# Gate products in seven-product form from output block 2 on, with the scaled sums of x made during attention in a buffer of their own

## The chip, the cores and the metric

The kernel runs on one core of one Trainium2 chip. The metric is the time of one execution on the device in microseconds (us). The five engines of a core (PE for matrix products, DVE and ACT for elementwise work, POOL for elementwise work and for issuing DMAs, SP for issuing DMAs) each work through a queue of their own in order and wait for each other by semaphores. Sixteen DMA engines move data between the core's memory and the device memory.

## The reference

One residual block of a streaming encoder, on x of 512 positions by 1024 channels, in float32:

```python
h = rms_norm(x, norm_mix_g[l])
proj = h @ w_in[l]
cb, cc, cin, q, k, v, f_logit, g_logit = jnp.split(proj, split_idx, axis=-1)
u = causal_dwconv(cc * cin, conv_mix_w[l])
y_conv = (cb * u) @ w_out_conv[l]
log_f = jax.nn.log_sigmoid((f_logit + b_f[l]).astype(jnp.float32))
o = forgetting_attention(q, k, v, log_f)
y_attn = o @ w_out_attn[l]
gates = jax.nn.sigmoid(g_logit + b_gate[l])
g_conv, g_attn = jnp.split(gates, 2, axis=-1)
x = x + (g_conv * y_conv + g_attn * y_attn) @ w_o[l]
h = rms_norm(x, norm_ffn_g[l])
up = causal_dwconv(h @ w_up[l], conv_ffn_w[l])
a, b = jnp.split(up, 2, axis=-1)
x = x + (jax.nn.silu(a) * b) @ w_down[l]
return rms_norm(x, norm_f_g)
```

The change touches `g_logit`, the last 2048 of the columns of `h @ w_in`: two gates for each of 1024 channels.

## The kernel before

Everything lies transposed: channels on the 128 partitions, the 512 positions along the free axis, so x is eight tiles of 128 by 512 (`KB` = 8). Each float32 operand is split into a high and a low part (`xgh` and `xgl` for x times the norm's gain, `wh` and `wl` for a weight block), and a product is three passes: high by high, low weight by high, high weight by low (`mm3`, L308). A pass over 128 by 512 outputs is two matmuls of 256 columns. The factor of the norm that depends on the position, `rb1`, is multiplied in when a result leaves PSUM.

The stages follow each other: the loads of x and of the v weights with the v product (a loop over the eight x tiles, `kb`), the q and k projections of two head pairs, attention (32 units of scores, softmax and transposes, with the remaining projections put between them as filler), the gate stage (a loop over eight output blocks `j`), the product with `w_o`, the channel mixer's up and down products and the last norm.

**The gate stage.** Output block `j` needs two gates of 128 channels each (`ga`, `gb`), the products `yc` and `ya` of the two branches (`chunk("mix…")`, 48 matmuls), and then gates times branches, which gives `mh` and `ml`. For `j` below `GJ` = 3 the two gates are two plain projections, 48 matmuls each (for `j` = 0 they were already made during attention). From `j` = 3 on the two gates of a block are one 2 by 2 block product with seven instead of eight block products (`seven`, L326): two steps of 42 matmuls. Such a step takes one load `P` of three weight blocks for each product pair, which come ready, and one load `F` of four sums of weight blocks. The sums are made in device memory by accumulating DMAs (`make_forms`): for each group of steps three copies issued on SP (L207) and three accumulations issued on POOL (L210), at counted slots during attention. `GATES` lists the steps, ten of them.

The seven products also need sums of x blocks. For these, x is loaded once more in float32 into `xt` (four DMAs of 512 KB on POOL's queue, L856). `x_scale` multiplies by the gain (ACT, L863), `x_sums` makes four sums and differences in place (DVE, L871 to L876), and `x_split` makes the high and low parts `xth` and `xtl` (ACT L882, DVE L883). These are entries of the list `later`: a piece with the index of a weight chunk from which it may run, an estimated DVE time and names by which a user can demand it. `split()` prepares the high and low parts of the next weight chunk (ACT L274, DVE L278), two chunks ahead of their use, and then runs pieces of `later` that fit a budget.

**Buffers.** The left side of the core's memory holds long-lived tiles, then `abp` (`xgh`, `xgl`, and the branch outputs). The right side holds `ap` during attention, and afterwards `xp`, `hp` and `mp` in the same place. The tag `x1` in `xp` is first `xt`; at `j` = 7 it becomes `x1`, x in float32 for the residual (four DMAs on POOL, L954), to which L1079 adds each block of the `w_o` product. The gates and their intermediate sums take turns in six buffers `mt`. PSUM has eight banks; `ring` hands out banks in turn, and `seven` takes four named ones.

**What sets the order.** Matmuls and instructions wrapped in `keep` stay in the order of the program. The rest is put in an order by the framework's scheduler, and each engine then runs its list strictly in that order, so a piece of work may stand at another place of an engine's list than the text suggests.

Of the kernel before, what the change touches and what calls it, by code (L numbers as in the profile page):

```python
# [8 lines left out]
F32 = mybir.dt.float32  # L9
F32R = mybir.dt.float32r  # L10
AF = mybir.ActivationFunctionType
ALU = mybir.AluOpType

P = 128
D = 1024
S = 512
KB = D // P
# [17 lines left out]
G1, G2, GF, BG, CM, CF, BF = 0, 8, 16, 24, 40, 52, 184  # L35
# [17 lines left out]
)  # L53
HELD = 2

GJ = 3
GATES = tuple(((j, q), (j, q + 1)) for j in range(GJ, KB) for q in (0, 2))

PLAIN = [(m, k) for m in (6, 7) for k in range(*PHASES[1])]
# [11 lines left out]
def block_kernel(ctx, tc, xT, vecs, wv, win, wmix, wo, wup, wst, wdp, outT):  # L71
# [3 lines left out]
    nc = tc.nc  # L75
# [25 lines left out]
    def col(i):  # L101
        return vec[:, i : i + 1]
# [22 lines left out]
    stream = [(f"v{kb}", wv[kb], S + H) for kb in range(KB)]  # L125
# [28 lines left out]
    raws, parts, order = [], [], {}  # L154
    pools = {"raw": wp}
    later = []
# [143 lines left out]
    def mm3(out, wh, wl, xh, xl, start, stop):  # L300


        n = out.shape[-1]
        cut = [slice(a, a + 2 * P) for a in range(0, n, 2 * P)] if n > 2 * P else [slice(0, n)]
        trio = ((wh, xh), (wl, xh), (wh, xl))
        for i, (w, x) in enumerate(trio):
            for c, cs in enumerate(cut):
                keep(nc.tensor.matmul(  # L308
                    out[:, cs], w, x[:, cs],
                    start=start and i == 0 and c == 0,  # L310
                    stop=stop and i == 2 and c == len(cut) - 1,
                ))
# [67 lines left out]
    otl = abp.tile([P, 4, S], F32R, tag="otl", name="otl")  # L380
    ych = abp.tile([P, 4, S], F32R, tag="ych", name="ych")
    ycl = abp.tile([P, 4, S], F32R, tag="ycl", name="ycl")

    at = ExitStack()
    ap = at.enter_context(tc.tile_pool(name="ap", bufs=1, side="right"))
# [61 lines left out]
    for kb in range(KB):  # L447
# [13 lines left out]
        for cs in cuts:  # L461
            keep(nc.vector.scalar_tensor_tensor(
                xgl[:, kb, cs], x[:, cs], col(G1 + kb), xgh.bitcast(F32)[:, kb, cs],
                op0=ALU.mult, op1=ALU.subtract,
# [33 lines left out]
    def proj(idx, name, evac, bank):  # L498
        st = {}

        def half(i):
            if i == 0:
                st["w"] = chunk(f"in{idx}")
                st["p"] = bank(f"p_{name}")
            wh, wl = st["w"]
            for kb in range(4 * i, 4 * i + 4):
                ks = slice(kb * P, (kb + 1) * P)
                mm3(st["p"], wh[:, ks], wl[:, ks], xgh[:, kb, :], xgl[:, kb, :], kb == 0, kb == KB - 1)
            if i == 1:

                while len(parts) < chunk.n + 2:
                    split()
                with after_split():
                    evac(st["p"])

        return [lambda: half(0), lambda: half(1)]
# [151 lines left out]
    def run_all(fs):  # L668
        for f in fs:
            f()  # L670
# [70 lines left out]
    run_all(proj(17, "k1", evac_qk(1, False), ring(1)))  # L741
    acc, bank_s, bank_t = ring(2, 0, 1), ring(3, 4), ring(5, 6)

    fill = []
    gp = []
    for idx in late:
        kind, i = divmod(idx, 4)
# [32 lines left out]
    def split_next():  # L780
        if len(parts) == chunk.n and stream[chunk.n][0] not in ("dp1", "dp2"):
            split()
# [38 lines left out]
            split_next()  # L821


    acc = ring(3, 4, 5, 6, 0, 1, 2, 7)
    xp = ctx.enter_context(tc.tile_pool(name="xp", bufs=1, side="right"))
    xt = xp.tile([P, KB, S], F32, tag="x1", name="xt")
    xth = xp.tile([P, KB, S], F32R, tag="x1h", name="xth")
    xtl = xp.tile([P, KB * S + PADR], F32R, tag="x1l", name="xtl")[:, : KB * S]
    xtl = xtl.rearrange("p (a b) -> p a b", b=S)

    hg = ExitStack()
    hp = hg.enter_context(tc.tile_pool(name="hp", bufs=1, side="right"))
# [5 lines left out]
    mp = mg.enter_context(tc.tile_pool(name="mp", bufs=1, side="right"))  # L838
    pools["rg"] = mp

    def mt(name):
        return mp.tile([P, S], F32, tag="mt", name=name, bufs=6)

    def evac_gate(idx, dst):
        def f(p):
            g = mt(f"g{idx}")
            nc.vector.tensor_mul(g, p, rb1)
            nc.scalar.activation(g, g, AF.Sigmoid, bias=col(BG + idx))
            dst.append(g)

        return f

    for q in range(4):
        nc.gpsimd.dma_start(xt[:, 2 * q : 2 * q + 2, :], xT[:, 2 * q : 2 * q + 2, :])  # L856
    xq = xt.rearrange("p (q b) (h c) -> p q (b h) c", b=2, h=2)
    xqh, xql = (t.rearrange("p (q b) (h c) -> p q (b h) c", b=2, h=2) for t in (xth, xtl))

    def x_scale(q):  # L860
        def f():
            for kb in (2 * q, 2 * q + 1):
                nc.scalar.activation(xt[:, kb, :], xt[:, kb, :], AF.Copy, scale=col(G1 + kb))  # L863

        return f

    def x_sums(qs):
        b11, b12, b21, b22 = (xq[:, qs, i, :] for i in range(4))

        def f():  # L870
            nc.vector.tensor_sub(b11, b11, b12)  # L871
            nc.vector.tensor_sub(b12, b22, b12)

        def g():
            nc.vector.scalar_tensor_tensor(b22, b11, -1.0, b22, op0=ALU.mult, op1=ALU.subtract)
            nc.vector.scalar_tensor_tensor(b21, b22, -1.0, b21, op0=ALU.mult, op1=ALU.subtract)  # L876

        return f, g

    def x_split(q):  # L880
        def f():
            nc.scalar.activation(xqh[:, q], xq[:, q], AF.Copy)  # L882
            nc.vector.tensor_sub(xql[:, q], xq[:, q], xqh.bitcast(F32)[:, q])  # L883

        return f

    k = [c[0] for c in stream].index("mix1")
    for q in (0, 2):
        f, g = x_sums(slice(q, q + 2))
        for i in (q, q + 1):  # L890
            later.append((k, 0, (("q", i),), x_scale(i)))
        later.append((k, 1.4, (("q", q),), f))
        later.append((k, 1.5, (("q", q),), g))
        for i in (q, q + 1):
            later.append((k + 1, 1.25, (("q", i),), x_split(i)))
        k += 2

    def gate_form(q, g):
        if g < 3:
# [47 lines left out]
    for j in range(KB):  # L947
        gs = []
        for _ in range(3):
            slot()  # L950
        if j == KB - 1:
            x1 = xp.tile([P, KB, S], F32, tag="x1", name="x1")
            for q in range(4):
                nc.gpsimd.dma_start(x1[:, 2 * q : 2 * q + 2, :], xT[:, 2 * q : 2 * q + 2, :])  # L954
        if j == 0:
            evac_gate(0, gs)(gp[0])
            evac_gate(8, gs)(gp[1])
        elif j < GJ:
            run_all(proj(20 + j, f"ga{j}", evac_gate(j, gs), acc))
            run_all(proj(28 + j, f"gb{j}", evac_gate(8 + j, gs), acc))  # L960
        else:
            if j == GJ:
                acc = ring(2, 7, 3, 4)
            seven(GATES[2 * (j - GJ) : 2 * (j - GJ) + 2], 2 * (j - GJ), {j: (0, 1, 5, 6)}, gate_form, done=gate_pair(j, gs))
        wh, wl = chunk(f"mix{j}")
        yc, ya = acc(f"yc{j}"), acc(f"ya{j}")
        for pp, hh, ll, o in ((yc, ych, ycl, 0), (ya, oth, otl, 4)):
            for k in range(4):
                ks = slice((o + k) * P, (o + k + 1) * P)
                mm3(pp, wh[:, ks], wl[:, ks], hh[:, k, :], ll[:, k, :], k == 0, k == 3)  # L970
        if j >= GJ:
            split_next()
            flush()
        a, b = gs
        nc.vector.tensor_mul(a, a, yc)
        nc.vector.tensor_mul(b, b, ya)
        nc.gpsimd.tensor_add(a, a, b)
        nc.scalar.activation(mh[:, j, :], a, AF.Copy)
        nc.vector.tensor_sub(ml[:, j, :], a, mh.bitcast(F32)[:, j, :])

    assert not todo_bg
    mg.close()
    ab.close()
    gx = ctx.enter_context(tc.tile_pool(name="gx", bufs=1))
    gx.tile([P, PADL], F32, tag="pad", name="pad_g")
    gh = gx.tile([P, NG, 2 * P], F32R, tag="gh", name="gh")
# [6 lines left out]
    acc = ring(0, 1, 5, 6, 3, 4, 2, 7)  # L993
# [80 lines left out]
    for j in range(KB):  # L1074
        slot()
        if j == 0:
            po = lead(["wo0", "wo1"], mh, ml)
        p = po[j] if j < 2 else block(f"wo{j}", mh, ml)
# [4 lines left out]
            op0=ALU.mult, op1=ALU.subtract,  # L1083
# [23 lines left out]
    acc = turns(0, 1, *(2, 3, 4, 5) * 2, 6, 7, 0, 1, 2, 3, 4, 5)  # L1107
# [185 lines left out]
    for ph, (j0, j1) in enumerate(PHASES):  # L1293
        if ph:
            flush()
            acc = turns(*X * 5)
# [211 lines left out]
```

## Time and profile before

| what | value |
|---|---|
| median of 3 runs | 696.33 us (696.13 to 696.6) |
| the profiled execution's own time | 695.75 us |
| its span, first to last instruction | 693.9 us |
| granted clock of PE in it | 0.998 |
| DVE, ACT, POOL busy | 531.4, 359.2, 178.3 us |

The span is 1.85 us shorter than the time of the same execution; what lies around it belongs to the launch. Sums below are made against the span and then carried to the median. In a profile, L with a number is a line of the kernel, `out<-in` names what is written and read, and the names of an engine with a small q (SPq, ACTq) are its queue of issues. A matmul row's duration is longer than the distance to the next matmul, because matmuls overlap; distances are read from starts or from counts in a window.

### The profile page before, as it was taken

The numbers are of one execution on the slowest core, as the hardware profiler recorded it, in microseconds if no ns is written. First come the engines' busy times: TensorE is split into PE (matmuls) and PEld (weight loads), VectorE is DVE, ScalarE is ACT, GpSimd is POOL, SyncE is SP. The second block draws the span as 40 slices with busy tenths as digits, with TensorE's granted clock in tenths as the row PEclk, the third lists the DMA queues.
The fourth block names the chain that finished last, engine by engine and source line by source line (L and its number), as shares of the span: only waits on it lengthen the run. The fifth ranks groups of instructions, "written<-read, shape, count | busy, mean of one in ns | idle before, by whom it ended". The sixth has DMA issues, their size and how long they took to land.

```text
span 693.9 us, 14635 instructions
## 1 busy us (share of the span) xinstructions
PE 686.2 (99%) x5972; PEld 684.6 (99%) x5972; DVE 531.4 (77%) x826; ACT 359.2 (52%) x565; POOL 178.3 (26%) x194
## 2 busy tenths in 40 slices
PE   9999999999999999999999999999999999999996
PEld 9999999999999999999999999999999999999996
DVE  6677877776577778768879799888774677777894
ACT  5665655644565444446554455545443344445572
POOL 4134846532221201113513134210000313222000
PEclk9999999999999999999999999999999999999999
DMA  7528988543698596766899776355646686776513
GB/s 256 158 70 272 197 200 193 129 91 92 223 263 244 166 269 193 207 217 141 114 316 294 201 178 135 116 177 176 201 128 232 141 195 157 188 169 172 164 31 122
DMA packets 58387, 124.68 MB, mean 180 GB/s; under 512 B 5280, under 2 KB 26800, under 8 KB 58320
## 3 DMA queue, kind: packets, MB, share of 16 engines
q1 hardware_dynamic: 40776, 99.68, 44.5%
q0 software_dynamic: 16304, 22.88, 20.9%
q10 hardware_dynamic: 1240, 1.19, 0.5%
q8 instruction: 47, 0.77, 0.4%
q14 instruction: 20, 0.16, 0.1%
HBM read 121.57 MB, written 39.32 MB: 232 GB/s over the span
## 4 chain that ended last, share of the span: by engine, by line
PE 96%; DVE 3%; issue 0%; ACT 0%; DVEq 0%
PE dn L326 24%; PE p_up L308 21%; PE p_in L308 14%; PE p_up L326 6%; PE p_wo L308 6%; PE yc L308 3%; PE ya L308 3%; PE pa L472 2%; PE pb L474 2%; PE p_q L308 2%; PE p_k L308 2%; PE p_gb L308 2%; PE p_ga L308 2%; PE o L653 2%; PE tp L636 1%; PE pdB L308 1%
## 5 line engine op out<-in xcount | busy, mean ns | idle before, releaser
L308 PE MATMUL p_up<-x1h,wh_up 128*128 128x256 f32 x464 | 90.5, 276 | 0.0
L308 PE MATMUL p_up<-x1h,wl_up 128*128 128x256 f32 x464 | 90.4, 276 | 0.0
L308 PE MATMUL p_up<-x1l,wh_up 128*128 128x256 f32 x464 | 90.3, 276 | 0.0
L308 PEld LDWEIGHTS p_up<-x1h,wh_up 128*128 128x128 f32 x464 | 69.9, 188 | 0.0
L308 PEld LDWEIGHTS p_up<-x1h,wl_up 128*128 128x128 f32 x464 | 69.9, 188 | 0.0
L308 PEld LDWEIGHTS p_up<-x1l,wh_up 128*128 128x128 f32 x464 | 69.8, 188 | 0.0
L274 ACT ACTIVATE wh_up<-raw_up 128x1024 fp32r<-128x1024 f32 x38 | 40.2, 1057 | 49.6 <-PE p_up L308 43.0
L210 POOL DMA_DIRECT2D f<-in_wst_dram x57 | 65.5, 1309 | 0.1
L278 DVE TENSOR_TENSOR wl_F<-raw_F,wh_F 128x1024 fp32r<-128x1024 f32 (+1 forms) x36 | 47.8, 1328 | 18.5 <-ACT wh_F L274 18.2
L308 PE MATMUL p_in<-xgh,wh_in 128*128 128x256 f32 x288 | 56.8, 279 | 0.0
L308 PE MATMUL p_in<-xgh,wl_in 128*128 128x256 f32 x288 | 56.6, 278 | 0.0
L308 PE MATMUL p_in<-xgl,wh_in 128*128 128x256 f32 x288 | 56.5, 278 | 0.0
L278 DVE TENSOR_TENSOR wl_up<-raw_up,wh_up 128x1024 fp32r<-128x1024 f32 x38 | 47.1, 1240 | 12.1 <-ACT wh_up L274 12.1
L274 ACT ACTIVATE wh_F<-raw_F 128x1024 fp32r<-128x1024 f32 (+1 forms) x36 | 37.9, 1053 | 35.4 <-PE dn L326 27.8
L1206 POOL TENSOR_TENSOR ge<-fu,fu 128x512 f32<-128x512 f32 x11 | 18.8, 1706 | 141.6 <-DVE fu L565 117.6
L274 ACT ACTIVATE wh_P<-raw_P 128x768 fp32r<-128x768 f32 (+1 forms) x36 | 30.0, 834 | 31.6 <-PE dn L326 22.3
L278 DVE TENSOR_TENSOR wl_P<-raw_P,wh_P 128x768 fp32r<-128x768 f32 (+1 forms) x36 | 35.0, 972 | 13.7 <-ACT wh_P L274 9.1
L308 PEld LDWEIGHTS p_in<-xgh,wh_in 128*128 128x128 f32 x288 | 44.7, 188 | 0.7
L326 PE MATMUL dn<-gl,wh_F 128*128 128x256 f32 x192 | 45.1, 276 | 0.0
L326 PE MATMUL dn<-gh,wh_F 128*128 128x256 f32 x192 | 45.1, 276 | 0.0
L308 PEld LDWEIGHTS p_in<-xgl,wh_in 128*128 128x128 f32 x288 | 43.7, 188 | 0.0
L308 PEld LDWEIGHTS p_in<-xgh,wl_in 128*128 128x128 f32 x288 | 43.6, 188 | 0.0
(349 smaller groups left out, 2148.5 us busy)
## 6 DMA issues: line engine op xcount, KB each, us to landing
raw_up<-in_wup_dram SPq DMA_DIRECT2D x38, 512.0 KB, 4.2
raw_F<-f SPq DMA_DIRECT2D x35, 512.0 KB, 4.5
raw_P<-in_wst_dram SPq DMA_DIRECT2D x35, 384.0 KB, 4.9
raw_in<-in_win_dram SPq DMA_DIRECT2D x26, 512.0 KB, 3.5
f<-in_wst_dram POOLq DMA_DIRECT2D x35, 256.0 KB, 6.4
f<-in_wst_dram SPq DMA_DIRECT2D x17, 512.0 KB, 5.7
f<-in_wst_dram POOLq DMA_DIRECT2D x17, 512.0 KB, 8.0
f<-f SPq DMA_DIRECT2D x34, 256.0 KB, 5.4
```

The source lines that it names most:

```text
L210: return lambda: keep(nc.gpsimd.dma_start(dst, src, accum_op=ALU.add))
L274: ins = nc.scalar.activation(hi, raw, AF.Copy)
L278: ins = nc.vector.tensor_sub(lo, raw, hi.bitcast(F32))
L308: keep(nc.tensor.matmul(out[:, cs], w, x[:, cs], start=start and i == 0 and c == 0, stop=stop and i == 2 and c == len(cut) - 1,))
L326: keep(nc.tensor.matmul(out, wl if x == 1 else wh, xl if x == 2 else xh, start=opens and bk not in seen, stop=closes and bk not in left,))
L472: keep(nc.tensor.matmul(pa[t][:, :VW], xt, w[:, VB:], start=start, stop=stop))
L474: keep(nc.tensor.matmul(pb[t], xt, w[:, :VB], start=start and t % 2 == 0, stop=stop and t % 2 == 1))
L636: keep(nc.tensor.transpose(tp[:, ks], pt[:, ks], ident))
L653: keep(nc.tensor.matmul(o[:, 2 * P * e + c0 : 2 * P * (e + 1)], w, x[:, kb, c0:], start=e == 0 and kb == 0 and i == 0, stop=e == 1 and kb ...
L1206: keep(nc.gpsimd.tensor_mul(ge, a.rearrange(halves_of, h=2), b.rearrange(halves_of, h=2)))
```

## The change

`GJ` goes from 3 to 2, so the two gates of output block 2 become two steps of seven products too (`GATES` now has twelve steps). `xt` gets a buffer of its own, 16 KB per partition in a new pool `yp` on the left side, open from before attention to the end of the gate stage. Its four loads and the pieces `x_scale` and `x_sums` are written ahead of attention, with chunk indices during attention; `x_split` stays behind attention and is set for the chunks of block 0. The place that was `xt` becomes `xm`, whose eight slices serve in turn as the gates' buffers instead of the six `mt`; since `x1` has the same tag, its loads now stand behind the gate loop. Two rings of PSUM banks are changed to go with it.

```diff
-GJ = 3
+GJ = 2
@@ -381,6 +381,10 @@
+    yg = ExitStack()
+    yp = yg.enter_context(tc.tile_pool(name="yp", bufs=1))
+    xt = yp.tile([P, KB, S], F32, tag="xt", name="xt")
@@ -740,6 +744,39 @@
+    for q in range(4):
+        nc.gpsimd.dma_start(xt[:, 2 * q : 2 * q + 2, :], xT[:, 2 * q : 2 * q + 2, :])
...
+    k = len(parts) + 2
+    for q in (0, 2):
+        f, g = x_sums(slice(q, q + 2))
+        for i in (q, q + 1):
+            later.append((k + i - q, 0, (("q", i),), x_scale(i)))
+        later.append((k + 2, 1.4, (("q", q),), f))
+        later.append((k + 3, 1.5, (("q", q),), g))
+        k += 4
@@ -821,12 +858,13 @@
-    acc = ring(3, 4, 5, 6, 0, 1, 2, 7)
+    acc = ring(3, 4, 5, 6, 2, 7)
-    xt = xp.tile([P, KB, S], F32, tag="x1", name="xt")
+    xm = xp.tile([P, KB, S], F32, tag="x1", name="xm")
@@ -839,7 +877,10 @@
-        return mp.tile([P, S], F32, tag="mt", name=name, bufs=6)
+        mt.n += 1
+        return xm[:, (mt.n - 1) % KB, :]
+
+    mt.n = 0
@@ -884,16 +900,9 @@
-    k = [c[0] for c in stream].index("mix1")
-    for q in (0, 2):
-        f, g = x_sums(slice(q, q + 2))
-        for i in (q, q + 1):
-            later.append((k, 0, (("q", i),), x_scale(i)))
-        later.append((k, 1.4, (("q", q),), f))
-        later.append((k, 1.5, (("q", q),), g))
-        for i in (q, q + 1):
-            later.append((k + 1, 1.25, (("q", i),), x_split(i)))
-        k += 2
+    k = [c[0] for c in stream].index("mix0")
+    for q in range(4):
+        later.append((k + q // 2, 1.25, (("q", q),), x_split(q)))
@@ -948,10 +957,6 @@
-        if j == KB - 1:
-            x1 = xp.tile([P, KB, S], F32, tag="x1", name="x1")
-            for q in range(4):
-                nc.gpsimd.dma_start(x1[:, 2 * q : 2 * q + 2, :], xT[:, 2 * q : 2 * q + 2, :])
...
-                acc = ring(2, 7, 3, 4)
+                acc = ring(3, 4, 2, 7)
@@ -980,7 +985,11 @@
+    yg.close()
     ab.close()
+    x1 = xp.tile([P, KB, S], F32, tag="x1", name="x1")
+    for q in range(4):
+        nc.gpsimd.dma_start(x1[:, 2 * q : 2 * q + 2, :], xT[:, 2 * q : 2 * q + 2, :])
```

The loads of `xt`, `x_scale` and `x_sums` stand in the second piece and leave their old place ahead of the fifth.

Where the scheduler puts the moved pieces is read from the order of each engine's list.

**POOL at the program's start**, where it clears the attention's operand tiles (`qb`, `kb`) and then waits to compute the norm's factor `rc_n`. Before:

```order
L527 MEMSET qb_110 4x512
L526 MEMSET kb_111 64x512
L525 MEMSET kb_112 4x512
L527 MEMSET kb_111 4x512
L526 MEMSET kb_112 64x512
L527 MEMSET kb_112 4x512
L355 TENSOR_TENSOR rc_n_415<-ms_n_413,ex 128x4
```

Now:

```order
L531 MEMSET qb_114 4x512
L530 MEMSET kb_115 64x512
L529 MEMSET kb_116 4x512
L531 MEMSET kb_115 4x512
L530 MEMSET kb_116 64x512
L749 DMA xt<-in_xT_dram 128x1024
L531 MEMSET kb_116 4x512
L749 DMA xt<-in_xT_dram 128x1024 x3
L355 TENSOR_TENSOR rc_n_419<-ms_n_417,ex 128x4
```

The four loads of `xt` stand among the clears, ahead of the norm's factor, in the stage that loads x and the v weights; no instruction in front of them waits for another engine there.

**POOL at the end of the gate stage**, where it adds the two gated branches of a block (`xm`, before `ga`), issues accumulations for the sums of the up weights (`f`) and then sums squares (`ssq`). Before, with the last rows of the stage:

```order
L210 DMA f_2593<-in_wst_dram 256x1x512
L954 DMA x_3803<-in_xT_dram 128x1024 x4
L977 TENSOR_TENSOR g_2928<-g_2928,g_2986 128x512
L977 TENSOR_TENSOR ga_3161<-ga_3161,gb_3166 128x512
L210 DMA f_2591<-in_wst_dram 256x1x256
L210 DMA f_2592<-in_wst_dram 256x1x256
L210 DMA f_2593<-in_wst_dram 256x1x256
L977 TENSOR_TENSOR ga_3351<-ga_3351,gb_3356 128x512
L977 TENSOR_TENSOR ga_3540<-ga_3540,gb_3545 128x512
```

Now:

```order
L210 DMA f_2618<-in_wst_dram 256x1x256
L982 TENSOR_TENSOR xm<-xm 128x512
L210 DMA f_2619<-in_wst_dram 256x1x256
L210 DMA f_2620<-in_wst_dram 256x1x256
L982 TENSOR_TENSOR xm<-xm 128x512
L992 DMA x_3982<-in_xT_dram 128x1024 x4
L1011 TENSOR_TENSOR ssq_3995<-ssq_3995,sq_1_4115 128x512
```

The loads of `x1` stood ahead of the addition for block 2 and now stand behind that for block 7, the last one; they write over `xm`, so they also wait for the last reader of `xm`, DVE's `ml`.

**DVE in attention**, at the second of the two places where it makes sums of x: `wl_in` is the low part of a projection's weights, `t_q` takes a projection out of PSUM, `ptl` is the low part of the transposed probabilities of a unit, read from the PSUM bank that the transposes of the unit after the next one need. Before:

```order
L278 TENSOR_TENSOR wl_in_1666<-raw_in_1344,wh_in_1665 128x1024
L538 SCALAR_TENSOR_TENSOR t_q_1669<-p_in_1580,rb_n_530 128x512
L640 TENSOR_TENSOR ptl_1562<-tp_1680,pth_1561 128x4x128
L619 RECIPROCAL m_1691<-m_1691 128x1
L551 TENSOR_TENSOR a_q_1671<-t_q_1669,a_q_1671 64x512 x2
```

Now:

```order
L278 TENSOR_TENSOR wl_in_1691<-raw_in_1361,wh_in_1690 128x1024
L763 TENSOR_TENSOR xt<-xt 128x2x256
L542 SCALAR_TENSOR_TENSOR t_q_1696<-p_in_1604,rb_n_534 128x512
L764 TENSOR_TENSOR xt<-xt 128x2x256
L644 TENSOR_TENSOR ptl_1586<-tp_1707,pth_1585 128x4x128
L555 TENSOR_TENSOR a_q_1698<-t_q_1696,a_q_1698 64x512 x2
```

Two subtractions of x blocks now stand ahead of this unit's `ptl`.

More of the change, by code (lines that the diff above doesn't have):

```diff
@@ L742, in block_kernel, with x_scale, f, x_sums @@
     acc, bank_s, bank_t = ring(2, 0, 1), ring(3, 4), ring(5, 6)
+    for q in range(4):
+        nc.gpsimd.dma_start(xt[:, 2 * q : 2 * q + 2, :], xT[:, 2 * q : 2 * q + 2, :])
+    xq = xt.rearrange("p (q b) (h c) -> p q (b h) c", b=2, h=2)
+    def x_scale(q):
+        def f():
+            for kb in (2 * q, 2 * q + 1):
+                nc.scalar.activation(xt[:, kb, :], xt[:, kb, :], AF.Copy, scale=col(G1 + kb))
+        return f
+    def x_sums(qs):
+        b11, b12, b21, b22 = (xq[:, qs, i, :] for i in range(4))
+        def f():
+            nc.vector.tensor_sub(b11, b11, b12)
+            nc.vector.tensor_sub(b12, b22, b12)
+        def g():
+            nc.vector.scalar_tensor_tensor(b22, b11, -1.0, b22, op0=ALU.mult, op1=ALU.subtract)
+            nc.vector.scalar_tensor_tensor(b21, b22, -1.0, b21, op0=ALU.mult, op1=ALU.subtract)
+        return f, g
+    k = len(parts) + 2
[6 more added lines that the diff above has]
+        k += 4
     fill = []
@@ L829, in block_kernel @@
     xtl = xtl.rearrange("p (a b) -> p a b", b=S)
+    xqh, xql = (t.rearrange("p (q b) (h c) -> p q (b h) c", b=2, h=2) for t in (xth, xtl))
     hg = ExitStack()
@@ L851, in evac_gate @@
         return f
-    for q in range(4):
[L856 to L878, printed above, removed]
     def x_split(q):
@@ L950, in block_kernel @@
             slot()
-        if j == KB - 1:
-            x1 = xp.tile([P, KB, S], F32, tag="x1", name="x1")
-            for q in range(4):
-                nc.gpsimd.dma_start(x1[:, 2 * q : 2 * q + 2, :], xT[:, 2 * q : 2 * q + 2, :])
         if j == 0:
```

## The prediction

> **What bounds the kernel now.** I read the page first, then PE's waits.
>
> ```profile
> span 693.9 us, 14635 instructions
> PE 686.2 (99%) x5972; PEld 684.6 (99%) x5972; DVE 531.4 (77%) x826; ACT 359.2 (52%) x565; POOL 178.3 (26%) x194
> PE 96%; DVE 3%; issue 0%; ACT 0%; DVEq 0%
> ```
>
> ```profile
> PE warm L115 <- DVE ones L107: 1.1, 1, 1.1
> PE p_up L326 <- DVE wl_up L278: 0.6, 1, 0.6
> ```
>
> PE is the chain that ends last, and it waits 1.7 us in all. So a matmul removed is worth its distance to the next one, work moved between other engines is worth nothing, and any wait that the change puts on PE is paid in full. A window over one plain pair of gates (`j` = 2), one step pair (`j` = 3) and the blocks from 3 to 7 gives the distance (the columns are length, then busy time and count of PE, PEld, DVE, ACT, POOL, then PE's clock, DMA share and GB/s):
>
> ```profile
> 203.88:214.76 10.88, 10.88 (x99) 10.88 (x97) 9.95 (x11) 7.83 (x10) 2.27 (x2) 1.00 0.78 177
> 220.20:229.72 9.52, 9.52 (x87) 9.52 (x85) 6.68 (x6) 5.28 (x6) 1.29 (x1) 1.00 0.88 303
> 220.20:295.00 74.80, 74.80 (x663) 74.80 (x661) 58.82 (x75) 35.11 (x45) 12.67 (x11) 1.00 0.72 216
> ```
>
> The counts hold three matmuls that overlap an edge. The last row is 5 blocks of 84 + 48 = 660 matmuls in 74.80 us, 113.3 ns each, without a gap; the page's 276 ns of one matmul is its duration, not its cost.
>
> **Term 1, the products of block 2.** Two projections are 96 matmuls, two steps 84. The first two rows are these two things: 10.88 - 9.52 = 1.36 us less, which is 12 times 113.3 ns. The end of block 2 costs DVE five sums where there was nothing before; PE has no wait in this stage, DVE is at 6.68 of 9.52 us beside a step pair, and the sums of x that filled it at block 2 (9.95 of 10.88) are gone, so this costs nothing (without that cover five sums of at most 0.69 us, 3.5 us). The splits of x now stand at the chunks of block 0, ahead of those of the steps; PE needs them at 203.9 and there are some 16 us of matmuls between (with no such lead the last of them would cost about 2 us, its ACT and DVE halves). The new loads `P` and `F` go out on SP in the places of `in22` and `in30`.
>
> **Term 2, the loads of xt at the start.** POOL's list puts them between and behind the last clears of `kb`. Here is when that is, and what the DMA engines and the v product do then:
>
> ```profile
> 9.05 0.52 POOL L526 MEMSET kb<- 64x512 f32 x1
> 9.63 0.52 POOL L527 MEMSET kb<- 4x512 f32 x1
> ```
>
> ```profile
> 9.18 3.91 SPq L182 DMA_DIRECT2D raw_v<-in_wv_dram  x4
> ```
>
> ```profile
> DMA packets 1399, 2.37 MB, mean 395 GB/s; under 512 B 159, under 2 KB 287, under 8 KB 1399
> q1 hardware_dynamic: 1399, 2.37, 106.2%
> raw_v<-in_wv_dram SPq DMA_DIRECT2D x4, 260.0 KB, 4.9
> ```
>
> ```profile
> 14.22 0.64 ACT L274 ACTIVATE wh_v<-raw_v 128x520 fp32r<-128x520 f32 x1 [0.57 <-PE pb L474]
> 14.77 0.71 ACT L453 ACTIVATE xgh<-xs,vec 128x512 fp32r<-128x512 f32 x1
> ```
>
> ```profile
> 16.89 0.28 PE L472 MATMUL pa<-wh_v,xgh 128*128 128x264 f32 x1
> ```
>
> The third fence is the window from 8 to 14 us: SP's queue q1 alone keeps all 16 engines full at 395 GB/s. The first xt load is issued at 9.57, the others by about 12.4. Its competitor is the first of the four weight loads, block 4 of the v product: issued at 9.18, landed 4.9 later at about 14.1, split from 14.22, ready with `xgh` at 15.48, used by PE at 16.89. So 1.4 us are to spare, and PE stands still if this load lands after 15.6. How the two queues share is seen at one place of this trace, where SP's 4 KB packets and POOL's met, in the window from 196 to 198 us:
>
> ```profile
> q0 software_dynamic: 98, 0.18, 53.4%
> q1 hardware_dynamic: 91, 0.36, 48.9%
> ```
>
> They take turns packet by packet. At the start an xt packet is 4 KB and a weight packet 2 KB, so q1 keeps about a third of its rate. An estimate of when xt's bytes begin: 512 KB take 1.3 us at 395 GB/s and a first load lands after 4.4 us (row below), so between 0 and 3.1 after the issue; I take 1.4, near 11.0. Where the weight load's own bytes end is an estimate too: 0.27 MB take 0.7 us at 395 GB/s, and by 14.0 the engines are about one and a half loads further, so near 12.9, and the rest of its way is the latency of the landing. The 1.9 us of transfers after 11.0 become 5.7 at a third of the rate, 3.8 later, less 0.1 for a slow beginning of xt: landed at 17.8. Ready 1.26 later, 19.1, against 16.89: **2.3 us** (2.2 by the rows and 0.1 for the semaphores). The next weight loads have 3 and more us to spare beyond that. Bounds: 0, if xt only gets what q1 leaves; 3.8, if all four xt loads go first (2.1 MB at 395 GB/s are 5.3 us). I take the middle, since the row on sharing shows turns. Nothing absorbs it: PE is in order and has no slack behind.
>
> **Term 3, the loads of x1.** They now wait for DVE's last `ml` of block 7:
>
> ```profile
> 298.56 0.68 DVE L979 TENSOR_TENSOR ml<-ga,mh 128x512 fp32r<-128x512 f32 x1
> 303.36 0.69 DVE L1079 TENSOR_TENSOR x<-p_wo,x 128x512 f32<-128x512 f32 x1 [4.12 <-PE p_wo L308]
> 304.50 1.23 DVE L278 TENSOR_TENSOR wl_wo<-raw_wo,wh_wo 128x1024 fp32r<-128x1024 f32 x1 [0.45 <-ACT wh_wo L274]
> ```
>
> ```profile
> 306.10 0.28 PE L308 MATMUL p_wo<-mh,wl_wo 128*128 128x256 f32 x1
> ```
>
> ```profile
> 298.66 0.33 SPq L182 DMA_DIRECT2D raw_wo<-in_wo_dram  x1
> 299.04 0.55 SPq L207 DMA_DIRECT2D f<-in_wst_dram  x1
> ```
>
> ```profile
> L856 POOL DMA_DIRECT2D xt<-in_xT_dram x4: 552/558/637, 185.6 to 187.3; - x4
> DMA to landing us min/median/max: 4.4/5.4/7.5
> ```
>
> ```profile
> L954 POOL DMA_DIRECT2D x<-in_xT_dram x4: 535/540/590, 215.5 to 217.1; - x4
> DMA to landing us min/median/max: 6.1/7.9/9.7
> ```
>
> Issued at 299.3, the first load lands after 4.4 us if alone and 6.1 beside other traffic: 303.7 to 305.4. DVE's addition of block 0 (303.36) waits for it, and right behind it in DVE's queue stands `wl_wo` of block 2, which PE needs at 306.10 and now has at 305.73. The addition and `wl_wo` take 1.9 us, so PE loses landing minus 304.2: 0 to 1.2 us. SP has two 512 KB transfers under way just then, so I take the upper row, **1.0 us** after rounding down for DVE's overlap.
>
> *By the Trainium skill*, "DMA: Bandwidth & Descriptors", section "Anatomy of one DMA — SWDGE (gpsimd) path", a DMA from POOL takes about 2.0 us plus its bytes at 436 GB/s; that would be an estimate of 3.2 us here, a landing at 302.5 and no loss, and the sum below would be 1.0 us smaller. The trace's rows of 4.4 and 6.1 us disagree, and they decide.
>
> **Term 4, the work moved into attention.** Eight ACT scalings and eight DVE sums move from the gate stage, where they cost nothing, and the splits move earlier within it:
>
> ```profile
> 194.16 2.55 ACT L863 ACTIVATE xt<-xt,vec 128x512 f32<-128x512 f32 x4
> 196.13 0.69 DVE L871 TENSOR_TENSOR xt<-xt 128x512 f32<-128x512 f32 x1
> 119.35 0.68 DVE L538 SCALAR_TENSOR_TENSOR t_q<-p_in,rb_n 128x512 f32<-128x512 f32 x1
> 119.95 0.68 DVE L640 TENSOR_TENSOR ptl<-tp,pth 128x512 fp32r<-128x512 f32 x1
> 121.95 0.27 PE L636 MATMUL tp<-ident,pp 128*128 128x128 f32 x1
> ```
>
> At the place shown in the order, two sums of 0.69 push `ptl` from 119.95 to about 121.3, done at 122.0, and the transposes that need its bank start at 121.95. That is 0.1 us; the other sums and the 0.64 us scalings meet spare times above 1.5 us. I take **0.1**, bounds 0 and 1.4 (one pair with no cover). One more group of weight sums adds three DMAs each to SP and POOL; each costs POOL 1 to 2 us of 178 busy, ahead of which the probabilities lie ready 4 us and more before PE's transposes: nothing.
>
> **The sum:** -1.36 + 2.3 + 1.0 + 0.1 = +2.0 us. The span goes to 695.9. The profiled run's time (695.75) is 0.6 under the median, and I carry the difference to the median: 696.33 + 2.04 = **698.4 us**.
>
> **The rivals.**
> - *The early traffic is mostly hidden.* q1's packets, queued first, get through, or x1 lands in time; one of terms 2 and 3 stays. For it: q1 has a full queue when xt arrives. Against: the turns above. Time: -1.36 + 1.0 + 0.1 = -0.3, 696.1; or -1.36 + 2.3 + 0.1 = +1.0, 697.4. Within 0.2%.
> - *The change does what it says and no more.* Both loads hide; 694.97 us, the full 1.36. It takes xt's bytes to leave the weight load before 15.6 and x1 to land by 304.2. For it: the unloaded 4.4 us; against: both landings would have to be at their best row. The gain is 0.195%, so half of this counts as faster.
> - *The long stall.* xt goes first: 3.8 + 1.2 + 0.1 - 1.36 = +3.7, 700.1, with a point of decision at a landing of 19.4. All rows show PE's clock at 1.00, so no row prices a slower one. The Trainium skill, "TensorE: Matmul & The Clock Gate", section "What's actually happening", says that PE's clock halves after an idle window of about 3.4 us; an estimate by that figure adds up to 2 us more here, and no run here shows it.
>
> **How the numbers follow.** Forecast (both stalls, net +1.4 to +3.2) 0.52; hidden in part 0.28; clean 0.12; long stall 0.08. A measurement of this kernel can tell about 0.2%, 1.39 us. Faster: half of the clean case and a little, 0.08. Same: the partial case, the other half and the forecast's lower edge, 0.32. Slower: 0.60. The range is 695.0 (clean) to 700.2 (long stall); the forecast's own is 697.6 to 699.5.
>
> **What would show it.** Right: the gate stage from 182 us loses 1.36 us with no gap; PE has a gap of 1.5 to 3 us at the start of block 4 of the v product, with ACT's `wh_v` waiting for `raw_v`; DVE's first `x<-p_wo` waits for the DMA of x and PE waits for `wl_wo` near 306. Wrong: no wait of PE on `wh_v` (term 2), the x addition released by PE as before (term 3), or PE waits in attention at units other than the one named (term 4).

## The result, and the profile after

| | median of 6 runs | lowest to highest |
|---|---|---|
| before | 696.41 us | 695.82 to 696.63 |
| changed | 699.02 us | 697.85 to 699.96 |

The changed kernel takes 1.0038 times as long, with a 95% interval of 1.0026 to 1.0051: slower by 2.6 us. The predicted time was 698.4 us. The changed kernel's profiled execution took 699.25 us, with a span of 697.5 us, so the two profiles are 3.6 us apart where the medians are 2.6 apart. Most of that 1 us is the kernel before: its profile (695.75 us) is of an execution 0.7 us below the median of 696.41, while the changed kernel's is 0.2 above its own.

The head of the page and PE's waits, of the changed kernel:

```profile
span 697.5 us, 14643 instructions
PE 686.2 (98%) x5960; PEld 684.0 (98%) x5960; DVE 534.6 (77%) x833; ACT 360.8 (52%) x568; POOL 181.7 (26%) x197
PE 88%; DVE 5%; ACT 2%; DMA 2%; issue 2%; POOL 0%; DVEq 0%; SPq 0%; ACTq 0%; POOLq 0%
```

```profile
PE p_wo L308 <- DVE wl_wo L278: 3.0, 1, 3.0
PE warm L115 <- DVE ones L107: 1.1, 1, 1.1
PE p_up L326 <- DVE wl_up L278: 0.6, 1, 0.6
PE pc_n L343 <- POOL ssq L1011: 0.3, 1, 0.3
```

PE has lost its 12 matmuls (5972 to 5960), but the chain that ends last is PE's to 88% only, where it was 96%. Two waits are new: one of 3.0 us in the `w_o` product and one of 0.3 us behind it. The gate stage and the `w_o` stage stand next to each other in windows from the first `yc` to the first `p_wo` and from there to the first `p_up` (columns as in the prediction). Before:

```profile
182.05:295.00 112.95, 112.95 (x999) 112.95 (x998) 87.95 (x110) 57.60 (x75) 22.75 (x24) 1.00 0.79 231
295.00:338.52 43.52, 43.52 (x387) 43.52 (x385) 34.12 (x41) 25.12 (x34) 12.50 (x10) 1.00 0.69 167
```

Changed:

```profile
182.62:294.21 111.59, 111.59 (x987) 111.59 (x986) 86.40 (x109) 54.62 (x70) 18.22 (x16) 1.00 0.73 204
294.21:341.00 46.79, 43.80 (x386) 43.61 (x385) 33.83 (x40) 24.94 (x34) 14.40 (x14) 1.00 0.76 199
```

The gate stage has 12 matmuls less and is 1.36 us shorter, with PE busy all the time. The `w_o` stage is 3.27 us longer with the same matmuls. Here is what PE, DVE and POOL do there (POOL's row is the four loads of `x1`):

```profile
305.09 0.39 PE L308 MATMUL p_wo<-mh,wh_wo 128*128 128x256 f32 x2
308.46 0.51 PE L308 MATMUL p_wo<-mh,wl_wo 128*128 128x256 f32 x2 [2.98 <-DVE wl_wo L278]
```

```profile
306.58 0.69 DVE L1088 TENSOR_TENSOR x<-p_wo,x 128x512 f32<-128x512 f32 x1 [8.14 <-DMA x<-in_xT_dram]
307.19 1.22 DVE L278 TENSOR_TENSOR wl_wo<-raw_wo,wh_wo 128x1024 fp32r<-128x1024 f32 x1
```

```profile
298.75 2.20 POOL L992 DMA_DIRECT2D x<-in_xT_dram  x4 [1.99 <-DVE ml L984]
```

Before, DVE's addition was released by PE at 303.36. Now it is released by the DMA of x at 306.58, after DVE has stood idle for 8.14 us, and `wl_wo` behind it is late for PE by 3 us.

The start of the program is also longer, by 0.5 us from the first v product to the norm's sums. It is lost before 9 us. The window from 4 to 9 us, before and changed:

```profile
4.00:9.00 5.00, 5.00 (x36) 4.91 (x36) 3.71 (x8) 2.26 (x4) 4.69 (x9) 1.00 0.91 287
```

```profile
4.00:9.00 5.00, 4.99 (x32) 4.80 (x32) 3.62 (x7) 2.15 (x4) 4.69 (x9) 1.00 0.84 272
```

PE has started four matmuls less by then, though the first load of `xt` is only issued at 9.53. From 9 us to the end of the v product both kernels take the same time within 0.02 us: block 4 has no gap. What remains (0.4 at the new `pc_n` wait, 0.4 in small steps in the up stage, 0.3 in the last norm) makes up the 3.6 us.

### The profile page after: what moved, and what is told of

The parts are those of the page before. It is cut to its first block, busy times and chain, and to the rows that moved or that the text cites. A ratio compares the mean times of both kernels' runs of the same rounds, so it can differ in the third digit from the quotient of the medians.

```text
span 697.5 us, 14643 instructions
## 1 busy us (share of the span) xinstructions
PE 686.2 (98%) x5960; PEld 684.0 (98%) x5960; DVE 534.6 (77%) x833; ACT 360.8 (52%) x568; POOL 181.7 (26%) x197
## 4 chain that ended last, share of the span: by engine, by line
PE 88%; DVE 5%; ACT 2%; DMA 2%; issue 2%; POOL 0%; DVEq 0%; SPq 0%; ACTq 0%; POOLq 0%
PE dn L326 25%; PE p_up L308 20%; PE p_in L308 14%; PE p_up L326 6%; PE yc L308 3%; PE ya L308 3%; PE pa L476 2%; PE pb L478 2%; PE p_q L308 2%; PE p_k L308 2%; PE o L657 2%; PE tp L640 1%; DMA x<-in_xT_dram 1%; PE pdB L308 1%; PE pdA L308 1%
## 5 line engine op out<-in xcount | busy, mean ns | idle before, releaser
L210 POOL DMA_DIRECT2D f<-in_wst_dram x60 | 71.0, 1352 | 1.3 <-DMA f<-f 1.0
L278 DVE TENSOR_TENSOR wl_F<-raw_F,wh_F 128x1024 fp32r<-128x1024 f32 (+1 forms) x38 | 51.0, 1343 | 19.0 <-ACT wh_F L274 18.9
L274 ACT ACTIVATE wh_F<-raw_F 128x1024 fp32r<-128x1024 f32 (+1 forms) x38 | 40.0, 1054 | 35.8 <-PE dn L326 26.6
L274 ACT ACTIVATE wh_P<-raw_P 128x768 fp32r<-128x768 f32 (+1 forms) x38 | 31.7, 834 | 35.5 <-PE dn L326 22.8
L278 DVE TENSOR_TENSOR wl_P<-raw_P,wh_P 128x768 fp32r<-128x768 f32 (+1 forms) x38 | 36.9, 971 | 16.3 <-ACT wh_P L274 10.6
```

The costliest lines, as they stand in the source:

```text
L210: return lambda: keep(nc.gpsimd.dma_start(dst, src, accum_op=ALU.add))
L274: ins = nc.scalar.activation(hi, raw, AF.Copy)
L278: ins = nc.vector.tensor_sub(lo, raw, hi.bitcast(F32))
```

## The experiments

Two theories. **A:** nearly the whole loss is the late landing of `x1`; the loads of `xt` cost nothing or little. **B:** the forecast's split, 2.3 us at the start and 1.0 us at `x1`. Each row below gives the ratio to the kernel before, run beside it on the same chip. The last column is read from the one execution that was profiled, and its time need not be the median: it was 695.25 us in x1_quiet, the shortest of ten, 698.15 in gj3, 702.87 in xt_sooner, 696.23 in sp_gj2 and 697.34 in sp_gj3.

| run | median us | before, us | ratio, 95% interval | PE's wait for `wl_wo` |
|---|---|---|---|---|
| x1_early | 695.04 | 696.08 | 0.9982 [0.9974, 0.9991] | none |
| xt_later | 698.46 | 696.08 | 1.0035 [1.0023, 1.0047] | 2.5 |
| both_moved | 695.42 | 696.08 | 0.9992 [0.9983, 1.0001] | none |
| gj3 | 699.33 | 696.08 | 1.0041 [1.0025, 1.0057] | 1.7 |
| x1_on_sp | 694.87 | 696.01 | 0.9984 [0.9975, 0.9994] | none |
| x1_quiet | 696.48 | 696.01 | 1.0006 [0.9996, 1.0016] | none |
| xt_sooner | 702.28 | 696.01 | 1.0085 [1.0070, 1.0101] | 2.3 |
| after_again | 698.83 | 696.01 | 1.0036 [1.0024, 1.0048] | 2.0 |
| sp_gj2 | 694.82 | 696.16 | 0.9983 [0.9974, 0.9992] | none |
| sp_gj3 | 696.76 | 696.16 | 1.0007 [0.9998, 1.0016] | none |

### x1_early: the loads of x1 in time

```diff
-    mt.n = 0
+    mt.n = 4
...
+        if j == KB - 1:
+            x1 = xm
+            for q in (0, 1):
+                nc.gpsimd.dma_start(x1[:, 2 * q : 2 * q + 2, :], xT[:, 2 * q : 2 * q + 2, :])
...
-    x1 = xp.tile([P, KB, S], F32, tag="x1", name="x1")
-    for q in range(4):
+    for q in (2, 3):
```

> Undoes the late loads of x1 alone: x1 is the same place as xm, the gates' buffers of the last block are its slices 4 to 7, so two of the four loads (blocks 0 to 3) are issued at the last block and only the other two behind the gate loop. Theory A (nearly the whole loss is the late landing of x1: 3.3 us between the first p_wo and the first p_up, knock-on after it 0.4): 695.3 to 695.9 us, 3.1 to 3.7 below the changed kernel; PE has no wait for wl_wo, DVE's first x<-p_wo is released by PE. Theory B (the forecast's split: 1.0 for x1, 2.3 at the start): about 698.0 us. Both fail if the four buffers left to the gates' sums at block 7 hold DVE up: then PE waits in the gate stage.

Measured: 695.04 us, 0.3 below theory A's range, 4.0 us below the changed kernel's 699.02 and 1.0 below the kernel before. (Each taken against the kernel before beside it, the two are 3.6 us apart.) The `w_o` stage takes 43.52 us again, and PE's waits are those of the kernel before:

```profile
PE warm L115 <- DVE ones L107: 1.1, 1, 1.1
PE p_up L326 <- DVE wl_up L278: 0.6, 1, 0.6
```

Theory A holds and B falls: undoing this part alone gives back more than the whole loss. The wait for `ssq` is gone too. Over all the profiles of this document it stands wherever DVE's first addition of x is late (seven), and nowhere else (five), so it is the same lateness passed on.

### xt_later: the loads of xt out of the start

```diff
-        nc.gpsimd.dma_start(xt[:, 2 * q : 2 * q + 2, :], xT[:, 2 * q : 2 * q + 2, :])
+        keep(nc.gpsimd.dma_start(xt[:, 2 * q : 2 * q + 2, :], xT[:, 2 * q : 2 * q + 2, :]))
...
-        nc.gpsimd.tensor_tensor(rc[:, :n], ms[:, :n], ex[:, :n], op=ALU.pow)
+        keep(nc.gpsimd.tensor_tensor(rc[:, :n], ms[:, :n], ex[:, :n], op=ALU.pow))
```

> Takes the four loads of xt out of the start and puts them on POOL's queue behind the norm's factor and the first rows of qb and kb, near 52 us; their first reader is at 72.7 us. Nothing else is moved. Theory A (the start costs 0.5 to 0.6 us): 698.4 to 698.6 us, the v stage (first product to the norm's sums) back at 21.3 us from 21.8. Theory B (the start costs 2.3 us): 696.7 us. A third way: the loads collide with the forms' traffic from 54 us on; then PE has a new wait in attention.

Measured: 698.46 us, which is A's number, though not by A's reason: the loads now start at 52.98, and the v stage still takes 21.86 us. So the 0.5 us of the start do not come from the loads of `xt` at all. At their old place these loads cost nothing in this comparison.

### both_moved

Both edits above together.

> Both edits, x1's loads early and xt's loads later. If the seven-product steps give 1.36 us and the two loads are all that was lost: 694.9 to 695.3 us, 1.1 to 1.5 below the kernel before and below the changed one by 3.7 to 4.1. If the gain of block 2 is taken back by something that neither load causes (the sums of x in attention, the rings of banks, the smaller number of buffers): 695.8 us or more.

Measured: 695.42 us, between the two bounds, and 0.4 above x1_early in the same series. Taking `xt` out of the start adds nothing to what x1_early gives; whether it costs a few tenths can't be told from these runs.

### gj3, and later sp_gj3: the steps alone

```diff
-GJ = 2
+GJ = 3
```

> The changed kernel with block 2 done by two plain projections again (GJ = 3), all else as changed. Every theory that takes the steps as pure product time: 12 matmuls of 113.3 ns more, +1.36 us, 700.2 to 700.5 us, the gate stage 111.6 us again and the same gap for wl_wo. Rival (the two more steps cost DMA traffic or buffers that show elsewhere): less than +0.7, at most 699.7 us.

Measured: 699.33 us, only 0.3 above the changed kernel, which by the total alone is the rival's number. The gate stage is 112.94 us, longer by the full 1.36 (the expectation's 111.6 is the changed kernel's figure). What differs is elsewhere: PE's wait for `wl_wo` is 1.7 us in this profile instead of 3.0, and the start has not lost its 0.5. That left the worth of the steps open, so the pair was run again in a kernel without the late `x1` (x1_on_sp, below).

> The kernel with x1's loads on SP's queue once more, beside the next one, on one chip: 694.6 to 695.2 us, 0.9 to 1.4 below the kernel before, no wait of PE for wl_wo.

> The same, with block 2 done by two plain projections (GJ = 3). With x1's loads in time neither kernel has the wait whose length changes from one execution to the next, so the difference of the two is the steps alone. Theory (12 matmuls of 113.3 ns): 1.36 us slower than its neighbour, 696.0 to 696.6 us, equal to the kernel before; the gate stage 112.94 us against 111.58, PE without a wait in it. Rival (the steps give less than their matmuls, because their loads, sums or buffers cost something elsewhere): less than 0.9 us between the two.

Measured: 694.82 and 696.76 us, 1.94 apart, the second 0.2 above its range. The rival falls. In the profiles the gate stages are 111.58 and 112.94 us, the second without a gap:

```profile
182.68:295.62 112.94, 112.94 (x998) 112.94 (x998) 82.27 (x102) 52.87 (x67) 18.20 (x16) 1.00 0.68 193
```

The other 0.6 us are more than the theory gave, and its premise did not hold: in the profile of sp_gj3 `x1` is late again, a little. DVE's first addition waits for the DMA (first row) and starts 0.6 us later after the first `p_wo` than in sp_gj2, where PE releases it, and PE waits for `ssq` in the up stage (second row), where it doesn't in sp_gj2.

```profile
304.51 0.69 DVE L1088 TENSOR_TENSOR x<-p_wo,x 128x512 f32<-128x512 f32 x1 [4.72 <-DMA x<-in_xT_dram]
```

```profile
PE pc_n L343 <- POOL ssq L1011: 0.2, 1, 0.2
```

The time from the first `p_up` to the end is 356.49 us against 355.45; of that 0.3 stand at this wait and 0.7 behind PE's last product. So the worth of the steps, 1.36 us, is shown by the gate stage; the difference of the totals is not the steps alone.

### x1_on_sp: the same late loads on another queue

```diff
-        nc.gpsimd.dma_start(x1[:, 2 * q : 2 * q + 2, :], xT[:, 2 * q : 2 * q + 2, :])
+        nc.sync.dma_start(x1[:, 2 * q : 2 * q + 2, :], xT[:, 2 * q : 2 * q + 2, :])
```

> x1's four loads stay behind the gate loop, with the same wait for the last reader of xm, but go out on SP's queue instead of POOL's; they stand there ahead of two copies of the forms and one w_o load, which now wait behind them. Theory Q (in the changed kernel the loads are late because POOL's queue gets its first packet only 3.4 us after the issue, while the engines work off what SP has queued): first landing near 302 to 303.5, before DVE's addition needs it at 304.2; no PE wait for wl_wo, 695.4 to 696.2 us. Rival (any load that starts at 298.5 is too late, by whatever queue): landing 305 or later, PE still waits 1 us or more, 697 us or more.

Measured: 694.87 us, 0.5 below the expected range and the whole loss gone, with the loads issued at nearly the same time (298.4 instead of 298.7) and behind the same wait. The first two, the only ones whose landing is recorded, land 3.9 and 4.8 us after the issue, where POOL's four landed after 7.7 to 9.8, and DVE's addition waits for PE again. From the view of the loads' line (duration, first and last issue, then the time to the landing), the changed kernel and x1_on_sp, and then DVE's addition in x1_on_sp:

```profile
L992 POOL DMA_DIRECT2D x<-in_xT_dram x4: 535/544/622, 298.7 to 300.4; - x4
DMA to landing us min/median/max: 7.7/8.7/9.8
```

```profile
L992 SPq DMA_DIRECT2D x<-in_xT_dram x4: 327/424/430, 298.4 to 299.7; - x4
DMA to landing us min/median/max: 3.9/4.4/4.8
```

```profile
302.47 0.69 DVE L1088 TENSOR_TENSOR x<-p_wo,x 128x512 f32<-128x512 f32 x1 [4.12 <-PE p_wo L308]
```

So 298.4 is not too late for the loads, though with little to spare: the first lands at 302.32, 0.15 us before the addition starts, and in the profile of sp_gj3 above it did not come in time. Whether POOL's queue made them late this run can't say by itself, because it changes the order as well: two copies of the forms and one `w_o` load stand behind `x1` on SP. The next run takes POOL's queue again and empties only SP's.

### x1_quiet: POOL's queue, with less queued on SP

```diff
+            late = 2 if key == 0 and g >= 3 else 0
-            todo_bg.extend((make_forms.slot + step * k + shift * g, op) for k, op in enumerate(ops))
+            todo_bg.extend((make_forms.slot + step * k + shift * g + (0 if k else late), op) for k, op in enumerate(ops))
```

> The changed kernel, but three copies of the forms on SP come two slots later, among them the one that SP issues at 298.25, just ahead of x1's loads; the w_o load of 512 KB at 297.87 stays. x1 is on POOL's queue as before. Theory Q (x1's first packet waits for what SP has queued, here 1 MB): half of that is gone, the first packet comes 1.5 to 2.2 us after the issue instead of 3.4, the first landing near 305 instead of 306.5, PE waits for wl_wo 0.8 to 1.8 us instead of 3.0; 697.0 to 698.0 us. Rival (a fixed latency of POOL's queue at this place): first packet still 3.2 us or more after the issue, the wait still 2.5 us or more, 698.4 to 699 us.

Measured: 696.48 us, 0.5 below the expected range. The profiled execution, 695.25 us, has no wait for `wl_wo` and a `w_o` stage of 43.81 us, 0.3 above the kernel before, which is more relief than expected; the longest of the ten took 697.91 us, and whether the wait stands in those is not shown. The queues' rows show the relief. In the changed kernel, from the issue at 298.75 to 302.1, there is traffic of SP's queue q1 and none of POOL's q0 (the first row); in x1_quiet, from 298.15 to 300, q1 moves half as much (second), and from 300 to 302 q0 has most of the engines' time (third and fourth).

```profile
q1 hardware_dynamic: 292, 0.83, 88.5%
```

```profile
q1 hardware_dynamic: 108, 0.44, 84.9%
```

```profile
q0 software_dynamic: 145, 0.56, 81.3%
q1 hardware_dynamic: 36, 0.08, 10.4%
```

POOL's first packet comes about 1.9 us after its issue instead of 3.4, and hardly anything shares the engines with it afterwards, so the first load lands after 4.7 us. DVE's addition still waits for it, but at 302.98, early enough for PE:

```profile
302.98 0.69 DVE L1089 TENSOR_TENSOR x<-p_wo,x 128x512 f32<-128x512 f32 x1 [5.13 <-DMA x<-in_xT_dram]
```

In this stretch one 512 KB copy of SP, issued 0.5 us ahead of `x1`, is all that SP has less. Between these two profiles it is the difference between a first packet after 1.9 and after 3.4 us, and between no wait for `wl_wo` and 3 us. In the four other profiles with that copy ahead (after_again, xt_later, xt_sooner, gj3) the first packet came 3.4 to 3.6 us after the issue. A fixed latency of POOL's queue is refuted.

### xt_sooner: does the start have a margin?

```diff
+        if t is KBt[0]:
+            for q in range(4):
+                nc.gpsimd.dma_start(xt[:, 2 * q : 2 * q + 2, :], xT[:, 2 * q : 2 * q + 2, :])
...
-    for q in range(4):
-        nc.gpsimd.dma_start(xt[:, 2 * q : 2 * q + 2, :], xT[:, 2 * q : 2 * q + 2, :])
```

> The four loads of xt stand three clears earlier on POOL's queue: first issue near 7.8 us instead of 9.5, all else as changed. Theory T (the queues do share packet by packet, as term 2 had it, but in the changed kernel xt's first bytes come at 12.3 us, when the weight load for block 4 is nearly through; so it costs nothing there): bytes begin near 10.6, the weight load for block 4 lands 3 to 4.6 us later than in the kernel before (17 to 18.7 instead of 14.1), PE stands still 1.4 to 3.1 us at block 4 of the v product, 700 to 702 us. Rival (SP's queue goes first whatever comes): no wait at block 4, at most 699.2 us.

Measured: 702.28 us, 0.3 above the expected range. Theory T holds. ACT's split of block 4 waits for its weights 5.1 us, and PE for ACT 3.0 (the second row is PE's first matmul of block 4):

```profile
19.17 0.64 ACT L274 ACTIVATE wh_v<-raw_v 128x520 fp32r<-128x520 f32 x1 [5.14 <-DMA raw_v<-in_wv_dram]
```

```profile
20.48 0.59 PE L476 MATMUL pa<-wh_v,xgh 128*128 128x264 f32 x1 [3.04 <-ACT xgh L457]
```

1.8 us earlier at POOL, and the stall of term 2 is there. In the changed kernel the same split is late as well, but not too late:

```profile
15.67 0.64 ACT L274 ACTIVATE wh_v<-raw_v 128x520 fp32r<-128x520 f32 x1 [1.44 <-DMA raw_v<-in_wv_dram]
```

It ends, with `xgh` behind it, at 16.92, and PE starts block 4 at 17.5. The margin is 0.5 us, and it doesn't always hold: the profiled execution of sp_gj2, the longest of its eleven with 696.23 us, has the split at 16.81 and PE waiting, here and again at block 5, 0.7 us in all:

```profile
16.81 0.64 ACT L274 ACTIVATE wh_v<-raw_v 128x520 fp32r<-128x520 f32 x1 [2.58 <-DMA raw_v<-in_wv_dram]
```

```profile
18.12 0.39 PE L476 MATMUL pa<-wh_v,xgh 128*128 128x264 f32 x1 [0.48 <-ACT xgh L457]
```

### after_again: what belongs to chance

The changed kernel, unchanged.

> The changed kernel once more, unchanged, on the same chip as the three others. Every theory: 698.4 to 699.2 us. It shows how much the wait of PE for wl_wo (3.0 us in its first profile, 2.5 and 1.7 in two kernels with the same late loads) and the first 9 us (0.5 us longer than in the kernel before) change from one execution to the next: if the 0.5 us belong to the change and not to chance, they stand here again.

Measured: 698.83 us. In this execution the wait for `wl_wo` is 2.0 us, the first 9 us are again 0.6 us longer, and there are two waits more of some length (and one of 0.2 us at the start):

```profile
PE p_wo L308 <- DVE wl_wo L278: 2.0, 1, 2.0
PE warm L115 <- DVE ones L107: 1.1, 1, 1.1
PE tp L640 <- DVE ptl L644: 0.8, 1, 0.8
PE pa L476 <- DVE wh_v L272: 0.7, 1, 0.7
```

The 0.8 us stand at 123.47 us, at the very `ptl` that term 4 named. The attention stage takes 130.55 us here and 129.58 in the first profile. The two sums ahead of this `ptl` use up its spare time, but they stand there in the first profile too; what comes on top here begins on POOL. One of its accumulations for the sums of weights waits for a copy of theirs:

```profile
112.35 1.11 POOL L210 DMA_DIRECT2D f<-in_wst_dram  x1 [1.04 <-DMA f<-f]
```

POOL's next addition (`y`), ACT's work on it (`ych`) and DVE's (`ycl`) come late by it, the last two by 1.07 us, and DVE brings this to the `ptl`. Of the eleven profiles with the new order in attention this is the only one with the wait.

The 0.6 us at the start are in both profiles of the changed kernel, but x1_quiet and gj3, which have the same start, don't show them, and sp_gj3 does. In the window from 4 to 9 us, x1_quiet and sp_gj3:

```profile
4.00:9.00 5.00, 4.96 (x36) 4.79 (x36) 3.74 (x8) 2.15 (x4) 4.69 (x9) 1.00 0.90 279
```

```profile
4.00:9.00 5.00, 5.00 (x32) 5.00 (x32) 3.59 (x8) 2.15 (x4) 4.69 (x9) 1.00 0.86 279
```

They come in two ways. In x1_early and sp_gj3 PE's first matmuls run 0.22 us apart instead of 0.12 until 7 us (until 5.4 in the kernel before). In after_again they don't, and PE stands 0.7 us for the second weight block instead (the row above); xt_later, which loads nothing of `xt` at the start, has the same wait with 0.4 us. Whether the change makes either more frequent is open; there is one profile of the kernel before, and its execution was 0.7 us shorter than the median beside the changed kernel.

## Why the prediction was right, and where it was not

The sign, the time (698.4 against 699.02) and the range held. The sum did not hold as it was put together: two terms were wrong and made up for each other, and that the total came out near the forecast is luck. (A slip on the way: the lower edge of the forecast's own range, 697.6, should be 697.7, 696.33 + 1.4.)

**Term 1, the products of block 2: right.** -1.36 predicted, 112.95 to 111.59 us measured, no gap, and 1.36 between the gate stages of sp_gj3 and sp_gj2. The five sums and the splits hide as said.

**Term 2, the loads of xt: 2.3 predicted, 0.0 measured** in both profiles of the changed kernel; the sign that the prediction set against this term, no wait of PE on `wh_v`, came true at block 4. The mechanism is real, as xt_sooner shows. The step that failed is the estimate of when xt's bytes begin: "I take 1.4, near 11.0". No packet of q0 appears before 12.3 us, 2.8 after the issue. Until then q1 alone has the engines, in the window from 9 to 12.2 us:

```profile
q1 hardware_dynamic: 764, 1.27, 105.3%
```

By the prediction's own working, with 12.3 in place of 11.0, 0.6 us of transfers become 1.8; the weight load would land 1.2 us late, near 15.3, inside the 1.4 us to spare. The bound of 0 was the right end, for that reason and not because q1 goes first. It was close: 0.5 us to spare in the changed kernel's first profile, and 0.7 us lost in the profile of sp_gj2.

**Term 3, the loads of x1: 1.0 predicted, 3.3 measured in the first profile and 2.3 in the second, and 0.4 passed on to `ssq`.** Place, order and mechanism were right: the addition waits for the DMA, `wl_wo` stands behind it, PE waits. The size was off because the landing was taken from rows of 4.4 and 6.1 us, and the first load took 7.7. The upper bound of 1.2 was no bound: the rows came from places where SP had less queued (0.19 and 0.51 MB moved by q1 before POOL's first packet, against 0.83). With 7.7 the prediction's formula gives 299.3 + 7.7 - 304.2 = 2.8. That SP had two 512 KB transfers under way was seen there, and used only to choose between the two rows. The Trainium skill, "DMA: Bandwidth & Descriptors", section "Anatomy of one DMA — SWDGE (gpsimd) path", gives an estimate of 3.2 us for this load; 7.7, 6.8 and, with an emptier queue, 4.7 us were measured, so the trace disagrees in every state of the queues seen here.

**Term 4, the work in attention: 0.1 predicted, 0.0 measured once and 1.0 once,** inside its bounds of 0 and 1.4, at the place named. The 1.0 needed something that the term put at nothing: POOL's work on the sums of weights. The wait of 1.04 us for one of their copies took what the two sums of x had left of the `ptl`'s spare time. Whether that copy is of the added group, the trace does not say.

**The rivals.** By its mechanism the rival "the early traffic is mostly hidden" came nearest: one of the two stalls stays. Its prices, 696.1 and 697.4, were wrong with term 3's size; with 3.3 + 0.4 the case that keeps `x1` gives -1.36 + 3.7 = +2.3 us, 698.7. "Does what it says and no more" is what x1_on_sp and sp_gj2 reach, 1.1 and 1.3 us below the kernel before. That version beats both kernels.

## What to carry to other kernels

A load on one queue need not begin when it is issued: at both places here POOL's got its first packet about 3 us later (2.8 and 3.4), while the engines worked off what SP's queue had been given. So count what is queued at the moment of issue, and take a landing only from a row with the same queue depth. Where a buffer is shared between its last reader and a load that is needed soon after, what stands ahead of the load decides: the same four loads cost 3 us on POOL's queue with two transfers of 512 KB from SP ahead of them, 0.3 us of the `w_o` stage in a profile with one, and nothing in two of three profiles on SP's queue ahead of the other transfers. And a stage whose gain is exact (1.36 us of 1.36) can still lose as a whole through a load that was moved out of its way.

## What the runs showed of the hardware

**The start of POOL's loads.** From issue to the first packet: 1.35 us at 185.6 in the kernel before, 2.8 at 9.5 and 3.4 at 298.75 in the changed one, 1.9 at 298.15 in x1_quiet. DVE was idle for the whole of the 3.4 us, so no work of DVE held POOL up. Once POOL's loads have started, both queues move packets side by side: from 302 to 304 us q0 and q1 have

```profile
q0 software_dynamic: 81, 0.33, 63.0%
q1 hardware_dynamic: 132, 0.24, 42.8%
```

**PE's clock after a gap.** In xt_sooner the gap at block 4, 3.33 us from start to start of PE's matmuls, is followed by matmuls 0.21 us apart for 3.4 us. The trace's record of the granted clock has it full from 6.71 us, half from 20.37 to 23.78, and full again. The full stretch of 13.65 us is four times 3.41, the half one is 3.41. The last of the four and the two behind it, in windows:

```profile
16.95:20.37 3.42, 0.48 (x5) 0.27 (x3) 0.53 (x1) 1.20 (x3) 0.00 (x0) 1.00 0.87 341
20.37:23.78 3.41, 3.31 (x15) 3.31 (x16) 3.31 (x6) 2.75 (x6) 0.00 (x0) 0.50 0.53 164
23.78:27.19 3.41, 3.41 (x30) 3.41 (x30) 2.10 (x5) 1.78 (x3) 0.00 (x0) 1.00 0.45 154
```

The v product is 4.8 us longer from 9 us on, 3.2 for the gap and 1.6 for the slow matmuls, which is why this run passed its expected range. The gap of 3.26 us at 308.46 in the changed kernel had no such sequel: its stage is longer by the gap alone. Counted in steps of 3.41 us from the start of full clock there (6.46), this gap lies across two stretches, and PE is busy for 2.06 and 1.79 us of them:

```profile
303.42:306.83 3.41, 2.06 (x19) 1.86 (x17) 0.25 (x1) 0.26 (x1) 0.00 (x0) 1.00 1.00 337
306.83:310.25 3.42, 1.79 (x15) 1.79 (x16) 3.29 (x6) 2.81 (x4) 0.00 (x0) 1.00 0.76 270
```

The Trainium skill, "TensorE: Matmul & The Clock Gate", section "What's actually happening", has the clock halved after an idle window of about 3.4 us that runs freely. The two cases agree with that: the gap that filled most of one stretch cost clock, the one of nearly the same length across two did not. Two cases can't show that the place and not the 0.07 us in length decides.
